# First column tile of a short-convolution layer: order of squares, low parts and scaling

## The chip, the cores and the metric

The kernel runs on one core of a Trainium2 chip. The metric is the device time of one execution in microseconds. The kernel before took 1109.05 us as the median of three runs (1108.74, 1109.05 and 1113.62). One more execution, recorded by the hardware profiler, took 1114.31 us; the rows below are from it.

## What is computed

A two-layer encoder step on 1088 tokens (1024 of a prompt, 64 of a running stream), with 1024 channels. The change lies in layer 0, the gated short convolution:

```python
h = rms_norm(x, norm_g[0])
b_gate, c_gate, xv, z = jnp.split(h @ w_in, 4, axis=-1)     # w_in: 1024 x 4096
u = c_gate * xv
conv = up[:, 0:T]*conv_w[0] + up[:, 1:1+T]*conv_w[1] + up[:, 2:2+T]*conv_w[2]   # up: two rows of state, then u
y = (silu(z) * b_gate * conv) @ w_out
```

Layer 1 is multi-head latent attention with a gate, and a last RMSNorm ends the step. Both come after the stretch that the change touches.

## The kernel before

Everything is held transposed: channels in the partitions, tokens in the columns. A float32 operand is split into a high part (rounded to the matmul's type, ACT) and a low part (source less high part); a product is three matmuls: high by high, high by low, low by high. Tokens come in two halves of 544 columns, and a half in two pieces, c=0 and c=1, of NS = 272 columns. The 4096 output columns of w_in are worked as eight column tiles `ct` of 128, each with four weight tiles of 128x1024, the parts, in the order 1, 2, 3, 0 (c_gate, xv, z, b_gate).

For the first half of the tokens, tiles 0, 1 and 2 are plain products (`conv_mm`, 24 matmuls for a part and a piece). `conv_mm` takes a `lag`: the matmuls with the weight's low part trail those with its high part by so many steps. From tile 3 on, two parts are taken together as a pair of seven block products of twelve matmuls (`Pair`, `prep`, `product`, `run`), which need sums and differences of the normalised x: `build(sc, k)` makes these, with VectorE and POOL for the first half (`sc` = 0, `build_first`) and POOL alone for the second.

The norm's factor is not applied to x before the first three tiles. x times the norm's gain is split (`x_split`), the squares of x are summed over the channels by `x_square` (ACT squares, VectorE adds into `rb`), and `rstd` sums `rb` over the partitions by TensorE (six matmuls of one column), takes the reciprocal root on VectorE in twelve small steps, and spreads it by TensorE (six matmuls of 128 columns); ACT copies it to `rb`, and `rb2` is its square. `finish_x` starts this and returns the rest of it. `conv_evac` scales a part by `rb2` or `rb` as it leaves PSUM; for the last part it goes on with `conv_tail`: three taps of the convolution in PSUM bank 7, then the gated result `y`, written to `y_scratch` by a DMA.

What sets the order: inside tile 0 ACT's, VectorE's and POOL's instructions that go through `ordered` are pinned behind what was traced before on their engine, and TensorE's matmuls are pinned from tile 0's first product on. DMAs (all on SP's queue), the weights of the next tiles, the builds and all that follows tile 0 on ACT, VectorE and POOL are placed by a scheduler that goes by the order of tracing and by when it takes an operand to be ready. Each engine then issues in that order. `side(n)` draws n steps from the list `jobs` (builds and `squares` of the second half): two after each piece in tiles 1 and 2, one after each block product in `run`.

PSUM has eight banks; `split_psum` deals them out and `gps` takes the next bank of a group in turn. In tile 0 group g has banks 0 to 6. A square goes to a buffer in SBUF (tags `kp6` and `cv`, the latter shared with `y`, one buffer each). The low parts of tile 0's weights are made by POOL. The scaling of piece c=0 stands behind the first product of c=1 as far as tracing goes, that of c=1 before tile 1. The second half's squares (`squares(k)` is four: channel tiles k and k+4 in two pieces, in two steps of two) go through bank 7: `squares(0)` and `squares(1)` in tiles 1 and 2, `squares(2)` and `squares(3)` ahead of `second_half` among the pairs. `second_half` lists at which of its 64 steps the second half's root and the four builds are drawn.

## Time and profile before

| | |
|---|---|
| median of three runs | 1109.05 us |
| profiled execution | 1114.31 us, its span 1112.5 us |
| PE busy | 1056.6 us (95%), 7123 matmuls |
| DVE, ACT, POOL busy | 749.8 (67%), 637.5 (57%), 539.7 us (49%) |
| PEclk in the first five of 40 slices | 8, 9, 9, 9, 8 tenths |
| DMA share in the first two slices | 7, 1 tenths |

PE is TensorE's matmuls, PEld its weight loads, DVE VectorE, ACT ScalarE, POOL GpSimd, SP the queue that issues the DMAs. Matmuls overlap at their ends, so PE's busy share is not the share of its peak. PEclk is the clock that TensorE was granted, as a share of the full one. In a timeline a row is: start, duration (of a run of like instructions from the first's start to the last's end), engine, line, operation, output and inputs, shapes, count, and in brackets the engine's idle time before it and what ended that.

### The profile page before, as it was taken

Reading aid. Unit: us, or ns where it says so; the run is one execution under the profiler, and the core shown is the slowest. Engines: PE = TensorE matmul, PEld = TensorE weight load, DVE = VectorE, ACT = ScalarE, POOL = GpSimd, SP = SyncE. Lnnn points to the kernel's source line nnn. Section 1 sums busy time; section 2 is a strip of 40 time slices with the busy share of each in tenths; the row PEclk is TensorE's granted clock in tenths of the full one; section 3 lists DMA queues with packets and bytes.
Section 4 is the critical chain, followed back from the end, with each engine's and each line's share of the span. In section 5 each row is a group of like instructions: output and inputs, shape, how many; then the busy total and the mean of one; then the engine's idle time right before and its main releaser. Section 6 shows DMA issues by size and latency. Waiting matters only on the chain.

```text
span 1112.5 us, 19655 instructions
## 1 busy us (share of the span) xinstructions
PE 1056.6 (95%) x7123; PEld 1010.2 (91%) x7123; DVE 749.8 (67%) x1516; ACT 637.5 (57%) x1388; POOL 539.7 (49%) x453
## 2 busy tenths in 40 slices
PE   8998899999999999999898999999999999999994
PEld 7888899999999999999798999899899999889983
DVE  6766577666666645564997432688888888896456
ACT  6445467666666533344532334777787777785352
POOL 3365399877666631221533321354555446463243
PEclk8999899999999999999999999999999999999997
DMA  7143234242322243422232104444323332334324
GB/s 233 59 136 107 82 115 141 86 164 77 114 96 96 95 140 131 139 82 87 92 122 98 51 31 107 100 98 96 83 57 88 86 74 49 100 124 152 93 83 153
DMA packets 58145, 114.55 MB, mean 103 GB/s; under 512 B 8080, under 2 KB 32400, under 8 KB 58048
## 3 DMA queue, kind: packets, MB, share of 16 engines
q1 hardware_dynamic: 57840, 112.97, 33.5%
q8 instruction: 56, 0.92, 0.4%
q14 instruction: 41, 0.34, 0.1%
q10 hardware_dynamic: 144, 0.26, 0.1%
q0 software_dynamic: 64, 0.07, 0.0%
HBM read 79.27 MB, written 16.31 MB: 86 GB/s over the span
## 4 chain that ended last, share of the span: by engine, by line
PE 66%; DVE 5%; issue 5%; POOL 4%; DMA 3%; ACT 3%; SPq 0%; POOLq 0%; ACTq 0%; DVEq 0%
PE PS L301 44%; PE PS L1459 17%; PE PS L1498 5%; DMA QB<-stg 2%; POOL wlo L1737 1%; DVE OL L983 1%; ACT PH L1511 1%; ACT stg L1575 1%; POOL t4l L632 0%; DMA wraw<-in_w 0%; POOL wlo L632 0%; SPq L1585 0%; DVE PL L1515 0%; DMA wraw<-in_wpair 0%; PE PS L1305 0%
## 5 line engine op out<-in xcount | busy, mean ns | idle before, releaser
L301 PE MATMUL PS<-R,whi 128*128 128x272 f32 (+2 forms) x1662 | 370.2, 312 | 16.6 <-DVE SZ L1003 5.2
L301 PEld LDWEIGHTS PS<-R,whi 128*128 128x128 f32 x1662 | 276.7, 191 | 21.5 <-ACT p L702 5.6
L301 PE MATMUL PS<-R,wlo 128*128 128x272 f32 (+2 forms) x888 | 266.7, 312 | 1.2 <-POOL wlo L292 0.9
L292 POOL TENSOR_TENSOR wlo<-wraw,whi 128x1024 fp32r<-128x1024 f32 x36 | 88.5, 2460 | 170.7 <-ACT whi L288 158.0
L301 PEld LDWEIGHTS PS<-R,wlo 128*128 128x128 f32 x888 | 165.1, 191 | 2.3 <-POOL wlo L292 1.7
L1459 PE MATMUL PS<-KB,QB 96*128 96x512 f32 (+11 forms) x576 | 126.6, 358 | 1.8 <-DMA QB<-stg 1.2
L1459 PEld LDWEIGHTS PS<-KB,QB 96*128 96x128 f32 (+1 forms) x576 | 95.5, 192 | 10.6 <-DMA QB<-stg 1.4
L1476 DVE TENSOR_REDUCE st<-PS 128x1 f32<-128x1024 f32 (+7 forms) x128 | 94.6, 748 | 13.1 <-PE PS L1459 12.3
L1493 POOL TENSOR_SCALAR Pt<-Pt,st 128x640 f32<-128x640 f32 (+3 forms) x64 | 61.4, 962 | 86.3 <-DVE st L1489 85.5
L1515 DVE TENSOR_TENSOR PL<-PS,PH 128x512 fp32r<-128x512 f32 (+3 forms) x192 | 98.7, 548 | 3.0 <-ACT PH L1511 1.6
L1511 ACT CAST PH<-PS 128x512 fp32r<-128x512 f32 (+3 forms) x192 | 85.4, 496 | 14.6 <-PE PS L1498 13.5
L1459 PE MATMUL PS<-PH,VB 128*128 128x256 f32 x320 | 76.4, 278 | 0.0
L632 POOL TENSOR_TENSOR wlo<-wraw,whi 128x1024 fp32r<-128x1024 f32 x26 | 62.4, 2401 | 26.7 <-ACT whi L631 24.0
L1459 PE MATMUL PS<-PL,VB 128*128 128x256 f32 x320 | 75.2, 281 | 0.2 <-DVE PL L1515 0.2
L1485 ACT ACTIVATE Pt<-PS,st 128x640 f32<-128x640 f32 (+3 forms) x64 | 62.1, 970 | 6.9 <-DVE st L1476 2.9
L301 PE MATMUL PS<-R,bhi 128*128 128x272 f32 x320 | 62.4, 293 | 2.3 <-DVE z L758 1.0
L1459 PEld LDWEIGHTS PS<-PH,VB 128*128 128x128 f32 x320 | 60.7, 190 | 1.3 <-DVE PL L1515 0.8
L1459 PEld LDWEIGHTS PS<-PL,VB 128*128 128x128 f32 x320 | 61.0, 190 | 0.7 <-DVE PL L1515 0.4
L288 ACT CAST whi<-wraw 128x1024 fp32r<-128x1024 f32 (+1 forms) x37 | 38.2, 1032 | 38.0 <-PE PS L301 20.4
L1498 PE MATMUL PS<-ident,Pt 128*128 128x128 f32 x416 | 55.4, 273 | 0.2 <-ACT Pt L1485 0.2
L301 PEld LDWEIGHTS PS<-R,bhi 128*128 128x128 f32 x320 | 50.5, 192 | 3.3 <-DVE u L758 1.4
L1493 POOL TENSOR_SCALAR Ph<-Ph,st 128x512 f32<-128x512 f32 (+3 forms) x64 | 34.0, 532 | 39.4 <-DVE st L1489 30.0
(438 smaller groups left out, 2649.9 us busy)
## 6 DMA issues: line engine op xcount, KB each, us to landing
wraw<-in_w SPq DMA_DIRECT2D x83, 512.0 KB, 3.5
KB<-stg SPq DMA_DIRECT2D x32, 256.0 KB, 3.8
QB<-stg SPq DMA_DIRECT2D x32, 256.0 KB, 5.1
braw<-in_w SPq DMA_DIRECT2D x13, 512.0 KB, 4.3
QB<-qr_scratch SPq DMA_DIRECT2D x32, 128.0 KB, 3.1
x<-x_scratch SPq DMA_DIRECT2D x8, 416.0 KB, 3.2
xr<-in_xT SPq DMA_DIRECT2D x16, 192.0 KB, 2.5
x_scratch<-xr SPq DMA_DIRECT2D x16, 192.0 KB, 1.8
```

What stands on the lines that cost most here:

```text
L288: ins = A.copy(out=hi[:, :n], in_=raw[:, :n])
L292: ins = (lo_engine or G).tensor_sub(lo[:, :m], raw[:, :m], r32(hi[:, :m]))
L301: ins = PE.matmul(ps, lhsT, rhs, start=start, stop=stop, skip_group_check=more)
L632: ins = eng.tensor_sub(lo, src, r32(hi))
L983: ordered((lo_engine or V).tensor_sub(lo, src, r32(hi)))
L1459: pin(PE.matmul(ps, lhsT, rhs, start=start, stop=stop))
L1476: pin(V.tensor_reduce(out=st[:, 0:1], in_=TL["S", h, i], axis=AX.XY, op=ALU.max, negate=True))
L1485: pin(A.activation(out=Pt, in_=TL.pop(("S", h, i)), func=AF.Exp, bias=st[:, 0:1], accum_out=st[:, 1:2]))
L1493: pin(G.tensor_scalar(Pt, Pt, st[:, 2:3], 1.0, op0=ALU.mult, op1=ALU.mult))
L1498: pin(PE.transpose(out=tp[:, j * P:(j + 1) * P], in_=TL["P", h, i][:, (j0 + j) * P:(j0 + j + 1) * P], identity=ident))
L1511: pin(A.copy(out=hi, in_=src))
L1515: pin(V.tensor_sub(lo, src, r32(hi)))
```

## The change

- The first tile's weights (all four parts) have their low part made by VectorE in place of POOL.
- A square of x goes to PSUM: bank group q (banks 6 and 7), and group g has banks 0 to 5. `rstd` in tile 0 uses q as well.
- Tile 0 is written out: the squares of c=0 are dealt between the casts of the third and fourth weight and after them; x of c=1 is loaded and split before any c=1 product; squares of c=1 come after the scaling of c=0's first two parts. The third product of c=0 and the fourth have the low parts at the end (lag KD).
- The spread of c=0 is put halfway into the second product of c=1 (`mid`), the scaling of c=0 comes in two portions behind it, and root, spread and scaling of c=1 (`rest`) come behind the first product of tile 1. Tile 1 takes its `u` and `z` after that.
- `y` has two buffers.
- `squares(2)` moves from the pairs to tiles 1 and 2; `squares(3)` has four steps of one square in place of two of two.
- The second half's root ends one step later, and its four builds start one step later at a spacing of 12 steps in place of 13.
- `os_` (attention, later) lies in pool pz in place of const.

```diff
--- before.py
+++ after.py
@@ -281,7 +281,7 @@
         if cuts:
             def part(a, b):
                 ordered(A.copy(out=hi[:, a:b], in_=raw[:, a:b]))
-                ordered(G.tensor_sub(lo[:, a:b], raw[:, a:b], r32(hi[:, a:b])))
+                ordered((lo_engine or G).tensor_sub(lo[:, a:b], raw[:, a:b], r32(hi[:, a:b])))
             return hi, lo, lambda a, b: SP.dma_start(out=raw[:, a:b], in_=src[:, a:b]), part
         dst = raw[:, :n] if view is None else view(raw[:, :n])
         SP.dma_start(out=dst, in_=src)
@@ -429,22 +429,22 @@
         return (STG, ST2)[k % 4 // 2][:, o:o + SC]
 
     def x_dma(c, k):
-        XS[k] = staged(k)[:, c * NS:(c + 1) * NS]
-        SP.dma_start(out=XS[k], in_=xT[k][:, c * NS:(c + 1) * NS])
+        XS[c, k] = staged(k)[:, c * NS:(c + 1) * NS]
+        SP.dma_start(out=XS[c, k], in_=xT[k][:, c * NS:(c + 1) * NS])
 
     def x_split(c, k):
         c0, c1 = c * NS, (c + 1) * NS
         g = sm[:, C_NG + k:C_NG + k + 1]
-        ordered(A.activation(out=HS[:, k, c0:c1], in_=XS[k], func=AF.Copy, scale=g))
-        ordered(V.scalar_tensor_tensor(LS[:, k, c0:c1], XS[k], g, r32(HS[:, k, c0:c1]), op0=ALU.mult, op1=ALU.subtract))
+        ordered(A.activation(out=HS[:, k, c0:c1], in_=XS[c, k], func=AF.Copy, scale=g))
+        ordered(V.scalar_tensor_tensor(LS[:, k, c0:c1], XS[c, k], g, r32(HS[:, k, c0:c1]), op0=ALU.mult, op1=ALU.subtract))
 
     def x_square(c, k):
         c0, c1 = c * NS, (c + 1) * NS
         if k == 0:
-            ordered(A.activation(out=rb[:, c0:c1], in_=XS[k], func=AF.Square))
+            ordered(A.activation(out=rb[:, c0:c1], in_=XS[c, k], func=AF.Square))
         else:
-            q = p1.tile([P, NS], F32, tag=("kp6", "cv")[k % 2], name=nm("sq"), bufs=1)
-            ordered(A.activation(out=q, in_=XS[k], func=AF.Square))
+            q = gps("q")[:, :NS]
+            ordered(A.activation(out=q, in_=XS[c, k], func=AF.Square))
             ordered(V.tensor_add(rb[:, c0:c1], rb[:, c0:c1], q))
 
     def load_x(c, ks=range(KD)):
@@ -455,7 +455,7 @@
 
     def finish_x(c):
         c0, c1 = c * NS, (c + 1) * NS
-        end = rstd([rb[:, c0:c1]], rb[:, c0:c1], D, NS)
+        end = rstd([rb[:, c0:c1]], rb[:, c0:c1], D, NS, tag="q")
 
         def rest():
             end()
@@ -463,12 +463,14 @@
 
         return rest
 
-    def conv_mm(c, W, lag=0):
+    def conv_mm(c, W, lag=0, mid=None):
 
         cs = slice(c * NS, (c + 1) * NS)
         wh, wl = W
         ps = gps()[:, :NS]
         for k in range(KD + lag):
+            if k == KD // 2 and mid:
+                mid()
             if k < KD:
                 mm(ps, wh[:, k * P:(k + 1) * P], HS[:, k, cs], k == 0, False)
                 mm(ps, wh[:, k * P:(k + 1) * P], LS[:, k, cs], False, False)
@@ -492,7 +494,7 @@
             A.activation(out=cv[:, s], in_=us[:, ct, 0:2], func=AF.Copy, scale=cw[0])
             for j in (1, 2):
                 V.scalar_tensor_tensor(cv[:, s], us[:, ct, j:j + 2], cw[j], cv[:, s], op0=ALU.mult, op1=ALU.add)
-        y = p1.tile([P, NS], F32, tag="cv", name=nm("y"), bufs=1)
+        y = p1.tile([P, NS], F32, tag="cv", name=nm("y"), bufs=2)
         ordered(V.tensor_mul(y, cv, z[:, a:b]))
         c0, c1 = sc * SC + a, sc * SC + b
         if sc == 0:
@@ -600,7 +602,10 @@
                 else:
                     A.activation(out=t, in_=q, func=AF.Square)
                     V.tensor_add(s, s, t)
-            yield
+                if k == 3:
+                    yield
+            if k < 3:
+                yield
 
     jobs = []
 
@@ -788,14 +793,14 @@
     PARTS = [1, 2, 3, 0]
     STD = 3
     pairs = [f for sc, cts in ((0, range(STD, KD)), (1, range(KD))) for ct in cts for f in conv_pairs(ct, sc)]
-    split_psum(g=(0, 7))
+    split_psum(g=(0, 6), q=(6, 8))
     ahead = []
     for ct in range(STD):
-        u, z = new_u(ct, 0), new_z()
         if ct == 0:
+            u, z = new_u(ct, 0), new_z()
             W = {}
             keep_order[0] = True
-            *w, dma, part = load_w(w1[ct][PARTS[0]], 1024, cuts=True)
+            *w, dma, part = load_w(w1[ct][PARTS[0]], 1024, lo_engine=V, cuts=True)
             W[PARTS[0]] = w
             dma(0, 256)
             x_dma(0, 0)
@@ -809,41 +814,58 @@
             part(640, 1024)
             for k in range(2, KD):
                 x_split(0, k)
-            *w, dma, part = load_w(w1[ct][PARTS[1]], 1024, cuts=True)
+            *w, dma, part = load_w(w1[ct][PARTS[1]], 1024, lo_engine=V, cuts=True)
             W[PARTS[1]] = w
             dma(0, 1024)
             part(0, 512)
             part(512, 1024)
             pe_order[0] = True
             held = {c: [] for c in range(2)}
-            held[0].append(conv_mm(0, W[1], 3))
-            for part, ks in ((3, range(4)), (0, range(4, KD))):
-                for k in ks:
+
+            def first(c, pi, lag=0, mid=None):
+                held[c].append(conv_mm(c, W[PARTS[pi]], lag, mid))
+
+            def evac(c, *pis):
+                for pi in pis:
+                    conv_evac(0, u, z, PARTS[pi], c, held[c][pi])
+
+            first(0, 0, 3)
+            for i, part in enumerate((3, 0)):
+                W[part] = load_w(w1[ct][part], 1024, lo_engine=V, into=[p1.tile([P, 1024], F32R, tag=x, name=nm(x), bufs=1) for x in ("bhi", "blo")] if part else
+                                 [R1[:, REG - n:REG - n + 1024] for n in (2048, 1024)])
+                for k in range(2 * i, 2 * i + 2):
                     x_square(0, k)
-                W[part] = load_w(w1[ct][part], 1024, into=[p1.tile([P, 1024], F32R, tag=x, name=nm(x), bufs=1) for x in ("bhi", "blo")] if part else
-                                 [R1[:, REG - n:REG - n + 1024] for n in (2048, 1024)])
-            for c in range(2):
-                for pi, part in enumerate(PARTS):
-                    if c or pi:
-                        held[c].append(conv_mm(c, W[part], (0, 6, 8, 0)[pi] if c == 0 else 0))
-                    late = c == 0
-                    if pi == 1 + late:
-                        n = 4 if late else 0
-                        if late:
-                            load_x(1, range(n))
-                        end = finish_x(c)
-                        if late:
-                            load_x(1, range(n, KD))
-                    if pi == 2 + late:
-                        end()
-                        for q in range(3):
-                            conv_evac(ct, u, z, PARTS[q], c, held[c][q])
-                    if pi == 3:
-                        conv_evac(ct, u, z, part, c, held[c][3])
+            first(0, 1, 6)
+            for k in range(KD):
+                x_dma(1, k)
+            for k in range(4, KD):
+                x_square(0, k)
+            first(0, 2, KD)
+            first(0, 3, KD)
+            for k in range(KD):
+                x_split(1, k)
+            end = finish_x(0)
+            first(1, 0)
+            first(1, 1, 0, end)
+            evac(0, 0, 1)
+            for k in range(4):
+                x_square(1, k)
+            first(1, 2)
+            for k in range(4, KD):
+                x_square(1, k)
+            evac(0, 2, 3)
+            first(1, 3)
+            end = finish_x(1)
+
+            def rest(u=u):
+                end()
+                evac(1, 0, 1, 2, 3)
+                conv_state(0, 0, u)
+
             keep_order[0] = False
-            split_psum(g=(0, 5))
+            split_psum(g=(0, 5), q=(7, 8))
             turns["g"][1] = 2
-            jobs.extend([build_first(0), build_first(1), squares(0), build_first(2), squares(1), build_first(3)])
+            jobs.extend([build_first(0), build_first(1), squares(0), build_first(2), squares(1), build_first(3), squares(2)])
         else:
             for pi, part in enumerate(PARTS):
                 W = ahead.pop() if ahead else load_w(w1[ct][part], 1024)
@@ -851,12 +873,18 @@
                     ahead.append(load_w(w1[ct + (pi == 3)][PARTS[(pi + 1) % 4]], 1024))
                     paced["lo"] = lo_on[0]
                 for c in range(2):
-                    conv_evac(ct, u, z, part, c, conv_mm(c, W, (KD, 0)[c]))
+                    ps = conv_mm(c, W, (KD, 0)[c])
+                    if ct == 1 and pi == c == 0:
+                        rest()
+                    if pi == c == 0:
+                        u, z = new_u(ct, 0), new_z()
+                    conv_evac(ct, u, z, part, c, ps)
                     side(2)
                 if ct == STD - 1:
                     with tc.issue_after(lo_on[0]), tc.issue_after(hi_on[0]):
                         step(0, (0, 1, 1, 4)[pi])
-        conv_state(ct, 0, u)
+        if ct:
+            conv_state(ct, 0, u)
     while jobs:
         side()
 
@@ -870,19 +898,19 @@
             todo.setdefault(t, []).append(f)
 
         def factors():
-            todo[8] = [rstd([rb[:, SC:]], rb[:, SC:], D, SC)]
+            todo[9] = [rstd([rb[:, SC:]], rb[:, SC:], D, SC)]
 
         at(3, factors)
         for k in range(4):
             steps = build(1, k)
-            for t in (0, 5, 6, 13):
-                at(10 + 13 * k + t, lambda steps=steps: next(steps, None))
+            for t in (0, 5, 6, 12):
+                at(11 + 12 * k + t, lambda steps=steps: next(steps, None))
         for t in range(64):
             for f in todo.get(t, []):
                 f()
             yield
 
-    jobs.extend([squares(2), squares(3), second_half()])
+    jobs.extend([squares(3), second_half()])
     step(1)
 
     pairs[2 * (KD - STD)].whole = True
@@ -1261,7 +1289,7 @@
 
     PSH = pS.tile([P, 5, 2 * P], F32R, name="PSH")
     PSL = pS.tile([P, 5, 2 * P], F32R, name="PSL")
-    os_ = const.tile([P, 8, DEC], F32, name="os_")
+    os_ = pz.tile([P, 8, DEC], F32, name="os_")
 
     WV, QA, PT, OL = {}, {}, {}, {}
```

## Rows read from the trace of the kernel before

**Rows 1.** Stretches: us, then busy us (instructions) by engine, clock, DMA share, GB/s.

```profile
12.80:45.85 33.05, 27.87 (x195) 26.83 (x194) 24.20 (x61) 17.44 (x38) 12.88 (x8) 0.90 0.40 136
45.85:97.35 51.50, 49.41 (x384) 48.30 (x385) 35.09 (x70) 23.83 (x44) 33.03 (x20) 1.00 0.38 114
97.35:121.30 23.95, 18.41 (x109) 17.75 (x108) 15.10 (x41) 10.04 (x21) 6.80 (x4) 0.79 0.29 101
131.00:223.00 92.00, 89.14 (x693) 88.29 (x692) 62.38 (x126) 61.65 (x119) 79.74 (x56) 0.98 0.33 116
150.00:200.00 50.00, 49.87 (x397) 49.61 (x396) 35.56 (x70) 35.23 (x68) 47.73 (x34) 1.00 0.39 130
```

**Rows 2.** Timeline, PE, first tile.

```profile
23.36 5.35 PE L301 MATMUL PS<-R 128*128 128x272 f32 x22 [1.55 <-POOL R L292]
...
35.66 0.72 PE L301 MATMUL PS<-ones,acc 128*128 128x1 f32 x6
...
41.43 0.93 PE L301 MATMUL PS<-ident,rsy 128*128 128x128 f32 x6 [1.93 <-DVE rsy L333]
```

**Rows 3.** PE's waits, 0 to 130 us: us in total, times, longest.

```profile
PE PS L301 <- ACT p L702: 3.9, 2, 2.8
PE PS L301 <- DVE rsy L333: 1.9, 1, 1.9
PE PS L301 <- DVE acc L602: 1.6, 1, 1.6
PE PS L301 <- POOL R L292: 1.5, 1, 1.5
PE PS L301 <- DVE acc L448: 1.2, 1, 1.2
```

**Rows 4.** Timeline, ACT and DVE, first tile.

```profile
11.91 1.14 ACT L283 CAST whi<-wraw 128x512 fp32r<-128x512 f32 x2 [2.09 <-DMA wraw<-in_w]
...
13.73 6.83 DVE L448 TENSOR_TENSOR acc<-acc,sq 128x272 f32<-128x272 f32 x7 [2.80 <-ACT sq L447]
...
25.82 0.15 DVE L323 TENSOR_SCALAR rsv<-PS 128x3 f32<-128x3 f32 x1
...
27.98 0.16 DVE L333 SCALAR_TENSOR_TENSOR rsy<-rst,rsy 128x3 f32<-128x3 f32 x1
```

**Rows 5.** Instructions by form, DVE, 0 to 42 us: count, busy us, mean ns, idle before.

```profile
L448 DVE TENSOR_TENSOR acc<-acc,sq 128x272 f32<-128x272 f32 x14 | 9.2, 659 | 3.4 <-ACT sq L447 2.8
```

**Rows 6.** Instructions by form, DVE, 42 to 98 us.

```profile
L602 DVE TENSOR_TENSOR acc<-acc,PS 128x272 f32<-128x272 f32 x6 | 2.6, 432 | 1.5 <-ACT PS L601 1.4
...
L563 DVE TENSOR_TENSOR R<-STG,R 128x544 fp32r<-128x544 f32 x2 | 1.4, 714 | 0.0
...
L574 DVE TENSOR_TENSOR R<-STG,R 128x272 fp32r<-128x272 f32 x2 | 0.9, 433 | 0.0
```

**Rows 7.** Instructions by form, POOL, 0 to 42 us.

```profile
L292 POOL TENSOR_TENSOR wlo<-wraw,whi 128x1024 fp32r<-128x1024 f32 x2 | 4.8, 2392 | 10.6 <-ACT whi L288 10.6
```

**Rows 8.** Timeline, first and last steps of the first half's builds.

```profile
43.18 0.78 DVE L568 SCALAR_TENSOR_TENSOR STG<-STG,sm,acc 128x544 f32<-128x544 f32 x1
...
89.43 1.38 POOL L563 TENSOR_TENSOR R<-ST,R 128x544 fp32r<-128x544 f32 x1 [3.02 <-ACT R L562]
```

**Rows 9.** Timeline, first pairs: DVE, ACT, PE.

```profile
104.64 0.44 DVE L496 TENSOR_TENSOR y<-PS,z 128x272 f32<-128x272 f32 x1 [2.45 <-DMA y_scratch<-y]
...
105.12 0.40 ACT L601 ACTIVATE PS<-ST 128x272 f32<-128x272 f32 x1 [3.57 <-DVE u L540]
106.02 0.40 ACT L601 ACTIVATE PS<-ST 128x272 f32<-128x272 f32 x1 [0.50 <-DVE acc L602]
...
107.69 0.58 PE L301 MATMUL PS<-R,whi 128*128 128x272 f32 x2 [2.82 <-ACT p L702]
```

**Rows 10.** Timeline, second half's builds: ACT and PE.

```profile
201.27 0.42 ACT L573 CAST R<-ST 128x272 fp32r<-128x272 f32 x1 [4.20 <-POOL ST L571]
...
205.91 0.52 PE L301 MATMUL PS<-R,whi 128*128 128x272 f32 x2 [1.80 <-ACT p L702]
```

## The prediction

> **What bounds the kernel now.** The busy shares (in the table) name TensorE, so the question is where TensorE loses time and who releases it. I read the stretches first [rows 1]. Between 150 and 200 us it runs 397 matmuls in 49.87 us, 0.126 us for one: that is the pace with nothing in the way. Three stretches are held against it.
> 12.80 to 45.85 us (first column tile from its second weight on): 195 matmuls, 168 of them long, 168 x 0.126 = 21.2 us; the other 27 are two sets of column sums and two of spreads at 0.72 and 0.93 us [rows 2] and the first three of the next tile, about 3.3 us. So 24.5 us of work stands in 33.05 us: 8.6 us lost.
> 45.85 to 97.35 us (tiles 1 and 2): 384 x 0.126 = 48.4 in 51.50: 3.1 lost.
> 97.35 to 121.30 us (first seven-product pairs): 109 matmuls, 99 long ones 12.5 us and ten sums about 0.8, so 13.3 in 23.95: 10.6 lost.
> The waits [rows 3] give the releasers. In the first tile: the accumulated squares (1.2 us), the low part of the fourth weight by POOL (1.5) and the reciprocal root of half c=1 (1.9). At the pairs: ACT's copies of finished products (3.9) and again the squares (1.6). The rest is clock: the 22 matmuls at 23.36 took 5.35 us, 0.243 each [rows 2], nearly twice the pace, behind 1.55 us of idle; between 97.35 and 121.30 the granted clock was 0.79 [rows 1]. Of the 10.6 us there 3.9 + 1.6 = 5.5 are waits, so 5.1 is clock: a wait costs about itself once more.
> After that the matmuls run at pace until the next stage, so what TensorE gains before 125 us is kept if nothing else becomes late.
>
> **First tile, 12.80 to 45.85 us.** The start stays: the second weight is cast at 11.91, after 2.09 us of waiting for its transfer [rows 4], and TensorE can't begin on it before about 12.6. x tiles of c=1 follow both later weights on SP's queue, as before, so no transfer is put ahead of one that is needed sooner.
> Squares: seven adds took 6.83 us from 13.73 [rows 4], 0.98 each, while POOL made low parts. The mean of all 14 is 0.659 us [rows 5]; the same sum with the square in PSUM (later in the kernel) takes 0.432 [rows 6].
> The Trainium skill (SBUF — State Buffer, Who interferes with whom) has it that a VectorE instruction with two SBUF inputs and a GpSimd one that reads SBUF exclude each other, and that one with a single SBUF input is free of it; the two rows agree. The rule also speaks against this change: low parts and the product for rb2 have two SBUF inputs, so the latter could stand behind a POOL low part of the next tile (2.39 us), and the sum below would be smaller by up to that.
> Low parts: POOL needs 2.39 us for 128x1024 [rows 7]. VectorE at that size isn't in the trace. 0.714 us for 544 columns and 0.433 for 272 [rows 6] make a slope of 1.03 ns a column, so 0.714 + 480 x 0.00103 = 1.21 us; bounds are 0.71 (544 columns) and 2.39 (POOL's). I take 1.21, the straight line. Two halves of the second weight and three pieces of the first cost VectorE about 2.9 us more together, the third and fourth weight 2.4.
> VectorE's queue then: second weight's low halves to 13.9, third's to 15.4, one add, fourth's to about 17.2, six adds to 19.8, eight low parts of x(c=1) at about 0.45 (the 272-column subtraction of [rows 6]) to 23.5. TensorE needs: second weight 12.8 to 15.8, third to 18.8, fourth to 21.8 (low parts from 20.8), sums to 22.5, then x(c=1) piece k at 22.5 + 0.38k against 20.3 + 0.45k. Nothing is late, so the 1.2, the 1.5 and the slow 22 matmuls (22 x 0.117 = 2.6 us) go. If VectorE needed 2.39 a low part, the fourth would end near 20.5 and the adds near 23.1: the sums 1.3 us late.
> The reciprocal root: from 25.82 to 27.98 [rows 4], 2.3 us on VectorE. For c=0 it runs under first(1,0) and half of first(1,1), 36 x 0.126 = 4.5 us: hidden. New wait: first(1,2) takes bank 0 again, which is free only after spread, copy, rb2 and the first scaling, some 0.2 + 0.4 + 0.45 + 0.45 behind the spread against 1.5 us of remaining matmuls: 0.6 us of wait with semaphores. For c=1 the sums come after first(1,3) and the spread after the next tile's first 24 matmuls (3.0 us). VectorE reaches that chain only behind the gated result of c=0 (a table load, SiLU, POOL's product, three taps), about 40.4 against 39.7: 0.8 us of wait. Queued behind the waiting VectorE steps are the scalings of c=1 and the first builds; TensorE has five banks, and asks for the first that they hold some 12 us later.
> So 24.5 + 0.6 + 0.8 = 25.9 in place of 33.05: **-7** (-3.3 to -8.5; the near end takes 1.3 for slow low parts and one POOL low part of 2.39 in front of rb2, as POOL stood in front of the adds in [rows 4]).
>
> **Tiles 1 and 2.** The builds of the first half need rb of c=1. Before, the first came at 43.18, 2.7 us ahead of tile 1, and the last of POOL's at 89.43 to 90.8 [rows 8], 6.5 us ahead of the pairs at 97.35. Now tile 1 starts near 36.7 and rb is there near 42: the builds stand some 8 us later against TensorE, and the second product, which needs the last of them, had 9 us to spare (about 99.9 less 90.8). Four squares of half two come in as well, 4 x 0.432 on VectorE and 4 x 0.40 on ACT. VectorE had 35.09 us of work in 51.50 [rows 1], some of it waiting for POOL, so there is room to catch up, but the cover is nearly used. Bounds: 0 (all hidden) and +8 (the chain of builds keeps its length). I take **+1.5**, near the free end because of the idle share.
>
> **First pairs, 97.35 to 121.30 us.** VectorE waited 2.45 us with y at 104.64 for the transfer of the y before (one buffer); ACT's next square waited 3.57 us behind it, more squares each for the add before, and the copy that TensorE needed came behind these: 2.82 us idle at 107.69 [rows 9]. With two buffers y doesn't wait. Four squares, not eight, are left, one a product (1.5 us) and not two (some 0.9 us each through one bank, from 105.12 to 106.02): they fit. The sums then find their adds done. What stays is the 1.07 us of the first copy (3.9 - 2.82), since in the first pair only one product lies between the two that use its bank, and perhaps 2 us for squares whose x arrives just in time. 10.6 - 1.1 - 2 = 7.5: **-7.5** (-3 to -9.5).
>
> **Half two's builds, 131 to 223 us.** POOL was busy 79.74 of 92 us [rows 1]; 16 low parts of 2.4 leave 41.3, 10.3 a build. At 13 products a build (19.7 us, with 8.9 of low parts) POOL just kept up; at 12 (18.1 us against 10.3 + 8.2 = 18.5) it falls behind by 0.4 a build, but ends three products sooner, before the next half asks. One such lag shows: ACT's cast waited 4.20 us for POOL, and TensorE 1.80 for a copy behind it [rows 10]. It may go or come twice: **+0.5** (-3.5 to +5). The later reciprocal root (one step) and os_ in another pool move no work: 0. Two y buffers let half two's POOL reads trail: 0 to -1, taken as 0.
>
> **Sum.** -7 + 1.5 - 7.5 + 0.5 = -12.5. The profiled execution took 1114.31 us (span 1112.5 and 1.81 around it), so its like would take 1101.8. The median of the three runs is 5.26 under it, so the forecast is 1109.05 - 12.5 = 1096.5 us.
>
> **Rivals.** (a) The builds keep their length, and the pairs wait for them at about the old hour: +8 in place of +1.5, -6, 1103. For: most of it is a chain over three engines. Against: VectorE's idle third. (b) The copies at the pairs stay late, now behind squares whose x is reloaded after the last build: -2 in place of -7.5, -7, 1102. For: ACT issues in order. Against: half the squares. (c) Both: -0.5, 1108.5. (d) The change doesn't do what it says in the first tile: the third and fourth weight land too late for TensorE and it idles as before, -1 for -7: 1102.5. Against: ACT before cast them behind waits for adds, not for transfers. (e) Slower: POOL over-full in half two's builds. Each cast that waits for POOL holds ACT's copies; one cost 1.8 us of wait and, by the ratio above, 1.7 of clock, 3.5. There are 16 such casts (four a build). From the sixth further one (6 x 3.5 - 12.5 = +8.5) the kernel is at 1117.5. For: 0.4 us a build too much; against: low parts are made a pair ahead.
>
> **Chances.** Forecast 0.56 (own range 1090 to 1101), (a) 0.13, (b) 0.11, (c) 0.08, (d) 0.06, (e) 0.06. The range takes in (a), (b) and (d) and reaches below the forecast for the full losses (-8.5 - 9.5 - 3.5): 1088 to 1106. About what a measurement of this kernel can tell from no change is 0.5%, 5.5 us: below 1103.5 lies the forecast and most of (a), (b) and (d): faster 0.77; same 0.16, (c) with the rest of these; slower 0.07.
>
> **What would show it.** First tile: adds at 0.43 each, no POOL low part before about 25 us, full clock from 13 to 40, next tile's first matmul near 37. Tiles 1 and 2: no wait for a build; the pairs' first matmul near 91. Pairs: no wait of y for a transfer, clock near 1.0 after. Builds: at most one or two waits for a copy. Wrong would be a first matmul of the pairs after 95, a slow clock behind it, or more than four waits for copies from 125 to 215.

## The result, and the profile after

The changed kernel took 1099.2 us (median of 7 runs, 1096.45 to 1102.93); the kernel before took 1114.73 on the same chip (7 runs, 1108.74 to 1116.55). The ratio is 0.9877, 95% interval 0.9845 to 0.9909: faster by about 1.2%. The profiled spans are 1097.4 and 1112.5 us, a difference of 15.1; the sum had said 12.5. From the median of 1109.05 that was shown ahead, the ratio gives 1095.4 us, beside the 1096.5 forecast. (1109.05 lay at the lower end of the runs before; in the later comparisons the kernel before has medians of 1109.86 to 1111.94.)

To see where the time came from, both traces are laid side by side by their matmuls. Each has 7123, issued in the same places of the program at the numbers below, so the start of the n-th one is a common clock:

```
n                                     after     before   after - before
72    (first tile, early)             15.41      16.01       -0.60
300   (tile 1 under way)              45.00      53.42       -8.42
624   (the pairs begin)               93.91      97.35       -3.44
800   (pairs' sums are done)         118.38     131.51      -13.13
1000                                 143.44     158.17      -14.73
1300                                 185.51     195.93      -10.42
1500  (half two's builds are done)   210.72     224.71      -13.99
7122  (last)                        1090.89    1106.01      -15.12
```

So the first tile gave 7.8 us (from -0.60 to -8.42), tiles 1 and 2 took 5.0 back, the pairs gave 9.7, half two's builds 0.9. The first 0.6 and the last 1.1 are not put down to the change: among the traces of this case the 72nd matmul starts anywhere from 14.81 to 17.80 us, with the landing of the first transfers and the clock behind it, and from the 3500th matmul (near 500 us) to the last the traces of the experiments below shift against that of the changed kernel by -1.9 to +6.1 us, though their edits lie before.

The stretches that answer to [rows 1], first tile, tiles 1 and 2, pairs, builds and the part of them at pace (us; busy us and instructions of PE, PEld, DVE, ACT, POOL; granted clock, DMA share, GB/s):

```profile
12.30:36.40 24.10, 23.46 (x187) 23.25 (x188) 17.96 (x44) 16.20 (x33) 5.55 (x3) 1.00 0.57 197
36.40:93.85 57.45, 51.67 (x391) 50.02 (x391) 46.89 (x93) 26.48 (x52) 35.75 (x20) 0.97 0.33 104
93.85:108.75 14.90, 13.43 (x108) 13.21 (x108) 13.34 (x34) 8.84 (x18) 6.90 (x4) 1.00 0.45 146
117.00:209.00 92.00, 88.90 (x700) 87.72 (x699) 63.49 (x128) 62.79 (x120) 79.72 (x56) 1.00 0.33 117
136.00:186.00 50.00, 46.90 (x365) 45.80 (x364) 32.72 (x67) 34.76 (x66) 44.72 (x34) 1.00 0.34 119
```

The first tile and the pairs stand at a granted clock of 1.00, where the pairs had 0.79, and TensorE fills them to nine tenths and more. The middle stretch is the one to read: 391 matmuls at 0.126 us are 49.3 us and it lasts 57.45, so 8.2 us are lost where 3.1 were. VectorE's busy time there went from 35.09 to 46.89 us, with 93 instructions for 70: root and scaling of c=1 and four more squares stand there now.

TensorE's waits to 130 us, against [rows 3] (us in total, times, longest):

```profile
PE PS L301 <- ACT whi L288: 4.4, 3, 2.8
PE PS L301 <- ACT p L707: 1.5, 1, 1.5
PE PS L301 <- POOL wlo L292: 1.2, 3, 0.5
...
PE PS L301 <- DVE u L528: 0.6, 1, 0.6
...
PE PS L301 <- DVE rsy L333: 0.2, 1, 0.2
```

All five waits of [rows 3] are gone but one copy and a short spread. Grown are the waits for a cast weight (`whi`, ACT; 1.0 us in two before) and for POOL's low part behind it (0.9 in two before). They stand in tiles 1 and 2. In the timeline (start, duration, instruction, in brackets the idle time before it and what ended it) TensorE, ACT, VectorE and POOL show this around the longest of them:

```profile
64.43 3.48 PE L301 MATMUL PS<-R,whi 128*128 128x272 f32 x16 [2.81 <-ACT whi L288]
...
60.01 0.42 ACT L575 CAST R<-ST 128x272 fp32r<-128x272 f32 x1 [4.85 <-DVE ST L570]
...
63.34 1.04 ACT L288 CAST whi<-wraw 128x1024 fp32r<-128x1024 f32 x1
...
53.31 1.60 DVE L576 TENSOR_TENSOR R<-STG,R 128x272 fp32r<-128x272 f32 x1
54.84 2.91 DVE L565 TENSOR_TENSOR R<-STG,R 128x544 fp32r<-128x544 f32 x1
57.67 1.60 DVE L579 TENSOR_TENSOR STG<-STG 128x272 f32<-128x272 f32 x1
59.20 0.77 DVE L570 SCALAR_TENSOR_TENSOR ST<-ST,sm,acc 128x544 f32<-128x544 f32 x1
...
53.10 1.52 POOL L565 TENSOR_TENSOR R<-STG,R 128x544 fp32r<-128x544 f32 x1 [4.15 <-ACT R L564]
54.59 2.57 POOL L292 TENSOR_TENSOR wlo<-wraw,whi 128x1024 fp32r<-128x1024 f32 x1
57.13 1.85 POOL L565 TENSOR_TENSOR R<-STG,R 128x544 fp32r<-128x544 f32 x1
```

Read it from the bottom. POOL works without a gap from 53.10 to 58.98 us. VectorE starts a two-input build step beside each of POOL's three instructions and each time ends it only 0.3 to 0.6 us behind POOL's end: 1.60, 2.91 and 1.60 us for sizes that took 0.43 and 0.71 [rows 6]. So the next build step (`ST`, L570) comes only at 59.20; ACT has waited 4.85 us for it; the next weight's cast is issued behind that build's copies on ACT and begins at 63.34; TensorE stands 2.81 us, and its next 16 matmuls run at 0.218 us each. The cast itself was ready long before: its weight had landed at 35.92, and the last matmul on the buffer that it writes ended at 55.6. What holds it is its place in ACT's order. In the stretch (instructions by form, count, busy us, mean ns):

```profile
L576 DVE TENSOR_TENSOR R<-STG,R 128x272 fp32r<-128x272 f32 x2 | 4.3, 2129 | 0.0
...
L565 DVE TENSOR_TENSOR R<-STG,R 128x544 fp32r<-128x544 f32 x2 | 3.6, 1813 | 0.0
```

Against [rows 6] (433 and 714 ns) these four instructions alone take 5.6 us more. Over all of VectorE's instructions that start between 36 and 92 us, the time beyond the shortest instruction of the same operation and shape (its excess, below) is 11.4 us; between 42 and 98 us of the kernel before it was 6.2 (the expectations below give 11.0 and 6.0).

In the first tile, POOL, DVE and PE show what was forecast, against [rows 2, 4, 5]:

```profile
16.72 3.14 DVE L448 TENSOR_TENSOR acc<-acc,PS 128x272 f32<-128x272 f32 x6
...
27.86 1.15 DVE L462 TENSOR_TENSOR rb2kp<-acc 128x272 f32<-128x272 f32 x1 [2.46 <-ACT acc L346]
...
26.33 2.39 POOL L292 TENSOR_TENSOR wlo<-wraw,whi 128x1024 fp32r<-128x1024 f32 x1 [25.01 <-ACT whi L288]
...
18.41 3.16 PE L301 MATMUL PS<-R 128*128 128x272 f32 x24
21.40 0.73 PE L301 MATMUL PS<-ones,acc 128*128 128x1 f32 x6
...
29.54 0.52 PE L301 MATMUL PS<-R,bhi 128*128 128x272 f32 x2 [0.64 <-DVE u L528]
```
```profile
L448 DVE TENSOR_TENSOR acc<-acc,PS 128x272 f32<-128x272 f32 x14 | 6.1, 436 | 1.2
...
L292 DVE TENSOR_TENSOR blo<-wraw,bhi 128x1024 fp32r<-128x1024 f32 x1 | 1.2, 1226 | 0.4 <-ACT bhi L288 0.4
```

The adds take 436 ns for 659, POOL's first low part comes at 26.33, the 24 matmuls at 18.41 run at the pace, and the column sums follow without a gap at 21.40. The wait at 29.54 is that of c=1's third product, `first(1, 2)`, for the scaling that stands right behind the product for `rb2` (L462).

At the pairs and in half two's builds, against [rows 9, 10]:

```profile
99.06 0.43 DVE L498 TENSOR_TENSOR y<-PS,z 128x272 f32<-128x272 f32 x1
...
98.55 0.52 PE L301 MATMUL PS<-R,t2h 128*128 128x272 f32 x2 [1.47 <-ACT p L707]
...
104.69 1.17 PE L301 MATMUL PS<-ones,acc 128*128 128x1 f32 x10
```
```profile
166.25 0.42 ACT L575 CAST R<-ST 128x272 fp32r<-128x272 f32 x1 [4.25 <-POOL ST L573]
...
170.87 0.52 PE L301 MATMUL PS<-R,whi 128*128 128x272 f32 x2 [1.87 <-ACT p L707]
```

`y` waits for no transfer, the sums find their adds done, and the one stall of the builds has moved from the fourth build (205.91) to the third (170.87) with nearly the same size.

### The profile page after: what moved, and what is told of

It is laid out like the page before. It is cut to its first block, busy times and chain, and to the rows that moved or that the text cites. A ratio compares the mean times of both kernels' runs of the same rounds, so it can differ in the third digit from the quotient of the medians.

```text
span 1097.4 us, 19670 instructions
## 1 busy us (share of the span) xinstructions
PE 1048.0 (95%) x7123; PEld 1003.3 (91%) x7123; DVE 754.0 (69%) x1523; ACT 638.3 (58%) x1388; POOL 532.1 (48%) x446
## 4 chain that ended last, share of the span: by engine, by line
PE 69%; DVE 10%; POOL 5%; issue 5%; DMA 4%; ACT 4%; SPq 1%; POOLq 0%; DVEq 0%; ACTq 0%
PE PS L301 48%; PE PS L1487 16%; PE PS L1526 5%; DMA QB<-stg 3%; POOL wlo L1765 1%; DMA wraw<-in_w 1%; POOL wlo L292 1%; DVE PS L488 1%; ACT PH L1539 1%; DVE OL L1011 1%; ACT stg L1603 1%; POOL R L565 1%; SPq L1613 1%; DVE PL L1543 0%; POOL R L513 0%
## 5 line engine op out<-in xcount | busy, mean ns | idle before, releaser
L1568 POOL TENSOR_TENSOR SZ<-SZ,ot 64x256 f32<-64x256 f32 x64 | 47.0, 746 | 11.7 <-DVE ot L1563 9.4
```

Of the source, the lines that this page charges most:

```text
L1568: pin(G.tensor_mul(sz, sz, TL.pop(("ot", h, pr))[rows]))
```

## The experiments

Each kernel is the changed kernel with the edit shown. Two measures are given: the ratio to the kernel before, measured beside it on the same chip (95% interval; the changed kernel itself stands at 0.9877), and, finer, how much later than in the changed kernel the n-th matmul starts, counted from n = 72 so that the first transfers drop out. In us, for the kernel before and for each run:

```
                   n=300    624    800   1500
kernel before       7.82   2.84  12.52  13.39
lo_pool             0.01   0.03  -0.04   0.00
sq_sbuf             3.30   1.50   1.47   1.51
lo_pool_sq_sbuf     4.15   4.12   4.06   4.07
scale_at_end        5.61   3.96   4.08   4.05
y_one               0.02   0.07   1.74   3.50
sq_pairs            0.00  -0.18   6.76   6.79
y_one_sq_pairs      0.00  -0.18   8.59  10.26
casts_first         0.02   0.38   0.42   0.44
builds_later        0.00  -1.35   6.59   6.75
spacing_13          0.29   0.28   0.76   1.51
no_low_read        -0.67  -7.60  -7.81  -7.75
low_halves          0.18  -0.86  -0.54  -0.53
```

Where an edit can't have acted yet (n = 300 for y_one, sq_pairs, y_one_sq_pairs and spacing_13), the rows differ by up to 0.3 us, so differences of that size are not read.

### First tile: low parts, squares, scaling

**lo_pool**, the low parts of the first tile back on POOL:
```diff
-            *w, dma, part = load_w(w1[ct][PARTS[0]], 1024, lo_engine=V, cuts=True)
+            *w, dma, part = load_w(w1[ct][PARTS[0]], 1024, cuts=True)
...
-                W[part] = load_w(w1[ct][part], 1024, lo_engine=V, into=...
+                W[part] = load_w(w1[ct][part], 1024, into=...
```


> The changed kernel with the first tile's low parts back on POOL; squares stay in PSUM and the order stays. Theory (the two-input conflict): adds read one SBUF operand and stay at 0.43 us, so POOL's low parts (2.39 us each) only hold up the low parts of x. The fourth weight's low part is then ready near 20 us against 20.8 needed: second sums (35.69 us in the changed kernel) 0.5 to 2 us later, total +0.5 to +2. Rival (POOL's speed itself was the loss, 1.5 us of wait and the slow clock behind it): the wait for POOL at the fourth weight comes back, second sums 4 us later or more, total +4.


Measured: 1098.33 us, ratio 0.9896 (0.9862 to 0.9929). The n-th matmuls stand within 0.04 us. With the squares in PSUM, POOL's low parts don't lengthen the adds:

```profile
L448 DVE TENSOR_TENSOR acc<-acc,PS 128x272 f32<-128x272 f32 x14 | 6.1, 437 | 6.6 <-ACT PS L447 5.4
```

Both expectations were too high: this part of the change is worth nothing by itself.

**sq_sbuf**, squares in SBUF, low parts still on VectorE:
```diff
-            q = gps("q")[:, :NS]
+            q = p1.tile([P, NS], F32, tag=("kp6", "cv")[k % 2], name=nm("sq"), bufs=(1, 2)[k % 2])
```


> The changed kernel with the squares of x written to SBUF as before (two tags), low parts on VectorE. Theory (conflict): no POOL instruction runs before 26 us, so the seven adds of piece c=0 keep 0.43 to 0.5 us and nothing moves before 29 us; the adds of c=1 (29.9 to 33.6 us) meet POOL's low part of the next tile (29.95 to 32.35) and end about 2 us later, which moves the second root and its spread (39.72 us) by 1 to 2 us: total +1 to +2. Rival (the buffers in PSUM were the gain): first sums (21.40 us) 2 us later or more.


Measured: 1101.55 us, ratio 0.9909 (0.9881 to 0.9937). The seven adds of c=1 take 5.72 us (timeline), one of them 2.46 beside POOL's low part of a weight of tile 1:

```profile
30.19 5.72 DVE L448 TENSOR_TENSOR acc<-acc,sq 128x272 f32<-128x272 f32 x7
```

and the spread of c=1 is late (TensorE's waits, us in total, times, longest):

```profile
PE PS L301 <- DVE rsy L333: 2.0, 1, 2.0
```

3.3 us at n = 300, of which tiles 1 and 2 absorb all but 1.5.

**lo_pool_sq_sbuf**, both edits.


> Both of the above in one: only the new order of the first tile is left of its edits. Theory (conflict): adds of c=0 run beside POOL's low parts again, 0.9 us each, first sums 3 us later or more than in the changed kernel, slow clock behind it, second sums 4 to 6 us later: more than the two alone together. Rival (order alone is the gain): second sums within 1.5 us of the changed kernel's.


Measured: 1103.13 us, ratio 0.9937 (0.9915 to 0.9959). 4.1 us, where the two alone make 0 + 1.5: the two edits meet on one conflict, and it takes both sides, an add with two SBUF inputs and a POOL instruction beside it. The timeline of the adds of c=0, and TensorE's waits for the spreads, now two:

```profile
15.94 6.58 DVE L448 TENSOR_TENSOR acc<-acc,sq 128x272 f32<-128x272 f32 x6 [0.73 <-ACT sq L447]
```
```profile
PE PS L301 <- DVE rsy L333: 4.1, 2, 2.2
```

Six adds take 6.58 us, as seven took 6.83 in [rows 4]. Either half of the change removes the conflict of c=0; only the squares in PSUM also remove that of c=1, where POOL belongs to the next tile. The new order, which is all that is left of the first tile's edits here, is worth 3.7 us at n = 300 (7.82 less 4.15).

**scale_at_end**, root, spread and scaling of c=1 at the end of tile 0:
```diff
+            rest()
...
-                    if ct == 1 and pi == c == 0:
-                        rest()
```


> The changed kernel with root, spread and scaling of c=1 put at the end of the first tile, ahead of tile 1's first product. Theory: TensorE waits for the root there, 36.4 to 39.5 us, so about 3 us less 0.2 that it waits now: tile 1's 24 first matmuls end 2.5 to 3 us later; total +1 to +3, since tiles 1 and 2 lose 6 us later to ACT's late weight casts and may lose less then. Rival: the order of the rest shifts with it and takes all of it back, 0.


Measured: 1103.39 us, ratio 0.993 (0.9906 to 0.9954). The spread then stands ahead of tile 1's first product on TensorE and waits for the root (TensorE's waits):

```profile
PE PS L301 <- DVE rsy L333: 3.3, 1, 3.3
```

5.6 us at n = 300, 4.0 kept, more than the 1 to 3 expected: a wait of 3.3 and the clock behind it (0.72 granted from 38 to 50 us). The deferral is the largest single piece of the first tile's gain.

### The pairs: `y` and the squares

**y_one**, one buffer for the gated result:
```diff
-        y = p1.tile([P, NS], F32, tag="cv", name=nm("y"), bufs=2)
+        y = p1.tile([P, NS], F32, tag="cv", name=nm("y"), bufs=1)
```


> The changed kernel with one buffer for y. Theory 1 (the wait of y for the transfer of the y before starts the stall at the pairs): the wait of about 2.4 us is back on VectorE near 101 us and TensorE idles 1.5 to 3 us behind it, with slow clock: total +3 to +5. Theory 2 (the number of squares between the copies makes the stall): y's wait is back, but TensorE loses less than 1 us.


Measured: 1102.36 us, ratio 0.9921 (0.9898 to 0.9944). y waits, and TensorE for a copy behind it (timeline, DVE and PE):

```profile
101.94 0.44 DVE L498 TENSOR_TENSOR y<-PS,z 128x272 f32<-128x272 f32 x1 [1.67 <-DMA y_scratch<-y]
...
104.09 0.52 PE L301 MATMUL PS<-R,whi 128*128 128x272 f32 x2 [1.15 <-ACT p L707]
```

1.7 us at the pairs, less than the first theory's 3 to 5 but with its wait. As much again is lost near 200 us, still among the first half's pairs, where y waits once more (1.65 us) and TensorE 1.48 for a scaling behind it.

**sq_pairs**, the squares of the second half at their old place and two a step, y with two buffers:
```diff
-                if k == 3:
-                    yield
-            if k < 3:
-                yield
+            yield
...
-            jobs.extend([..., squares(1), build_first(3), squares(2)])
+            jobs.extend([..., squares(1), build_first(3)])
...
-    jobs.extend([squares(3), second_half()])
+    jobs.extend([squares(2), squares(3), second_half()])
```


> The changed kernel with squares(2) and squares(3) ahead of the second half's steps as before, two squares a step; y keeps two buffers. Theory 1: the stall at the pairs stays away, total 0 to +2 there, and tiles 1 and 2 lose up to 1 us less without squares(2). Theory 2: ACT's copies stand behind two squares a product again, TensorE waits 3 us or more with slow clock, the pairs' first 100 matmuls take 19 us or more in place of 14.9: total +4 to +6.


Measured: 1106.34 us, ratio 0.9945 (0.9926 to 0.9965). 6.8 us, all at the pairs. PE's timeline, and the stretch in the columns of the first fence:

```profile
108.97 1.97 PE L301 MATMUL PS<-ones,acc 128*128 128x1 f32 x10 [3.15 <-DVE acc L604]
```
```profile
93.85:116.00 22.15, 17.36 (x112) 16.71 (x111) 15.72 (x41) 9.96 (x21) 7.41 (x4) 0.85 0.31 109
```

This is the second theory, and somewhat beyond its size. TensorE waits chiefly for the last add, ahead of the column sums, less for copies (1.6 us, for 1.5 in the changed kernel); the mean clock is 0.85 where it was 1.00.

**y_one_sq_pairs**, both edits.


> Both undone: the pairs as before, the first tile as changed. By either theory the 9 us at the pairs come back, in part or whole (pairs' first 100 matmuls near 24 us in place of 14.9), total +5 to +9; if they do not come back, the pairs' gain came from the first tile's shift and not from these two edits.


Measured: 1107.87 us, ratio 0.9978 (0.9958 to 0.9997). 8.6 us at n = 800, the sum of the two (1.7 + 6.8). Counted from n = 624 it is 8.8 of the 9.7 us that the pairs gained; 0.9 is not accounted for by these two. With both edits undone TensorE's waits here are again chiefly for copies (3.5 us in two, 1.7 for the last add), as in [rows 3].

### Tiles 1 and 2: why 5 us came back

**casts_first**, the weight's cast issued ahead of the build steps on ACT:
```diff
-                    paced["lo"] = lo_on[0]
+                    paced["lo"], paced["hi"] = lo_on[0], hi_on[0]
```


> An addition to the changed kernel: in tiles 1 and 2 the ACT instructions of builds and squares are issued behind the cast of the weight that was loaded ahead. Theory (the 6 us lost in tiles 1 and 2 come from casts of weights queued on ACT behind build steps that wait for VectorE): waits of TensorE for these casts (4.4 us now) and for the low parts behind them (1.2) fall under 1.5 us together, the pairs start 3 to 6 us earlier (near 89 to 91 us in place of 93.9), total -2 to -6. Rival (the builds themselves are the bound): the casts come earlier, but the pairs wait for builds, total within 1 us.


Measured: 1100.86 us, ratio 0.9909 (0.9889 to 0.9929), 0.4 us slower by the matmuls, about what can't be read. The expected 2 to 6 us didn't come: TensorE still waits for casts (and 2.0 us, for 1.2, for the low parts behind them), and ACT now stands idle in front of SiLU for VectorE's scaling (TensorE's waits from 39 to 95 us, then two lines of ACT's timeline):

```profile
PE PS L301 <- ACT whi L288: 3.0, 2, 2.3
```
```profile
61.42 0.43 ACT L533 ACTIVATE z<-z 128x272 f32<-128x272 f32 x1 [5.55 <-DVE z L532]
...
63.50 1.04 ACT L288 CAST whi<-wraw 128x1024 fp32r<-128x1024 f32 x1
```

VectorE is late here too. But the theory isn't refuted: the edit holds back only steps that are drawn after the weight's load, and the cast at 63.50, only 0.5 us earlier than in the changed kernel (counted from n = 72), still stands behind that SiLU, two build casts and two squares drawn before it. Its weight had landed at 36.80 and its buffer was free at 56.35, so it could have run in ACT's 5.55 us of idle time. A cast put ahead of that SiLU was not tried.

**no_low_read**, the low parts of the weights of tiles 1 and 2 left out: POOL writes zeros of the same size in their place, and so reads no SBUF:
```diff
-        ins = (lo_engine or G).tensor_sub(lo[:, :m], raw[:, :m], r32(hi[:, :m]))
+        ins = G.memset(r32(lo[:, :m]), 0.0) if zero else (lo_engine or G).tensor_sub(...)
```


> The changed kernel, but the low parts of the weights of tiles 1 and 2 are left out: POOL writes zeros there and reads no SBUF for them (these tiles' products are of lower precision). Theory (the 6.6 us lost in tiles 1 and 2: VectorE's two-input build steps stand still beside POOL's low parts, 11.0 us over their shortest durations between 36 and 92 us against 6.0 before, which makes the scalings late and ACT's SiLU and weight casts behind them): that excess falls under 5 us, TensorE waits under 1.5 us there and the pairs start 4 us earlier or more. Rival (VectorE has too much work or a bad order, POOL or not): the casts are still waited for, the pairs start less than 2 us earlier.


Measured: one run, 1089.68 us. The stretch from n = 300 to 624 shrinks by 6.9 us; first VectorE's and POOL's instructions by form (36 to 92 us), then TensorE's waits (36 to 98 us), then a line of VectorE's timeline in the first tile:

```profile
L576 DVE TENSOR_TENSOR R<-STG,R 128x272 fp32r<-128x272 f32 x2 | 2.0, 1022 | 0.0
...
L565 DVE TENSOR_TENSOR R<-STG,R 128x544 fp32r<-128x544 f32 x2 | 1.4, 714 | 0.0
...
L292 POOL MEMSET wlo<- 128x1024 f32 x6 | 5.7, 953 | 3.1 <-PE PS L301 3.1
```
```profile
PE PS L301 <- ACT whi L288: 1.3, 1, 1.3
```
```profile
28.47 0.44 DVE L462 TENSOR_TENSOR rb2kp<-acc 128x272 f32<-128x272 f32 x1 [2.49 <-ACT acc L346]
```

The 544-column step is back at 714 ns, one of the two 272-column steps is still long (mean 1022), and the waits for low parts are gone. So POOL's making of low parts, beside the builds, is what these 7 us hang on. How is less clear. VectorE's excess is 6.2 us, not under 5 as expected, and no less than in the kernel before. The zeros also cost POOL less than half (953 ns, for 2542 in the changed kernel) and don't wait for the cast, so this run alone doesn't say whether VectorE's standing still or POOL's own queue counts for more.

The run also settles a point of the first tile. With no POOL low part beside it the product for `rb2` takes 0.44 us for 1.15, the wait of `first(1, 2)` (0.64 us) is gone, and the 300th matmul comes 0.67 us earlier.

**low_halves**, the same low parts in two instructions of 512 columns each:
```diff
+        for a in range(0, m, m // pieces):
+            b = a + m // pieces
+            ins = (lo_engine or G).tensor_sub(lo[:, a:b], raw[:, a:b], r32(hi[:, a:b]))
...
-                W = ahead.pop() if ahead else load_w(w1[ct][part], 1024)
+                W = ahead.pop() if ahead else load_w(w1[ct][part], 1024, pieces=2)
```


> The changed kernel with POOL's low parts of the weights of tiles 1 and 2 made in two instructions of 512 columns (1.39 us each by the rows of the kernel before) in place of one of 1024 (2.39). Theory (a VectorE build step stands still until the POOL instruction beside it ends): the step waits for half as long; the excess over the shortest durations between 36 and 92 us falls from 11.0 to about 8, the weight casts come 2 to 3 us earlier, pairs start 1.5 to 4 us earlier, total -1 to -4. Rival (POOL and VectorE take turns, so the total of both stays and POOL is the later one): VectorE's excess falls, but TensorE waits for the low parts instead, total within 1 us or slower.


Measured: 1099.74 us, ratio 0.9894 (0.9873 to 0.9915), 0.9 us earlier at n = 624 and 0.5 at n = 800, where 1.5 to 4 was expected. The two forms that stood still longest are short again (2129 and 1813 ns in the changed kernel), but others stand still more (the first line below, 1088 ns in the changed kernel), and the excess falls only from 11.4 to 8.5 us. First VectorE by form (36 to 92 us), then TensorE's waits, which hardly fell (36 to 98 us):

```profile
L572 DVE SCALAR_TENSOR_TENSOR ST<-ST,sm,acc 128x544 f32<-128x544 f32 x4 | 5.9, 1474 | 0.0
...
L578 DVE TENSOR_TENSOR R<-STG,R 128x272 fp32r<-128x272 f32 x2 | 2.0, 987 | 0.0
...
L567 DVE TENSOR_TENSOR R<-STG,R 128x544 fp32r<-128x544 f32 x2 | 1.4, 718 | 0.0
```
```profile
PE PS L303 <- ACT whi L288: 4.1, 3, 2.4
...
PE PS L303 <- POOL wlo L294: 1.6, 1, 1.6
```

It doesn't beat the changed kernel by more than can be measured.

**builds_later**, the builds' steps held back beside the first weight of tile 1 (both products):
```diff
-                    side(2)
+                    if ct > 1 or pi:
+                        side(2)
```


> The changed kernel with the first four build steps (two draws beside tile 1's first part) drawn one part later; 26 steps have 28 places. Theory (builds that are traced early but ready late stand ahead of the scalings on VectorE): the scaling of tile 1's third part, 7.6 us late now, comes within 3 us of its product, the wait of 2.8 us for the weight cast goes, pairs start 2 to 5 us earlier. Rival (the builds' own length is the bound): waits move to the end of tile 2 or to the first pairs, total within 1.5 us.


Measured: 1107.47 us, ratio 0.997 (0.9949 to 0.999). The pairs begin 1.35 us earlier and then lose 7.9: one copy is 4.8 us late there (TensorE's waits from 95 us on, then the last build step on VectorE):

```profile
PE PS L301 <- ACT p L707: 4.8, 1, 4.8
```
```profile
93.19 1.91 DVE L565 TENSOR_TENSOR R<-ST,R 128x544 fp32r<-128x544 f32 x1
```

The rival had the place right, the first pairs, and the size wrong: 6.6 us at n = 800 and not within 1.5. The run mixes two things. The last build step ends 1.7 us behind the pairs' first matmul, where POOL's last ended 6.5 us ahead of it in the changed kernel; and `squares(2)` slips among the pairs with the builds, so that eight squares stand there and not four, as in sq_pairs, which lost 6.8 us without any late build. So what late builds cost by themselves is not shown.

### Half two's builds

**spacing_13**, root and builds of half two at the old steps:
```diff
-            todo[9] = [rstd([rb[:, SC:]], rb[:, SC:], D, SC)]
+            todo[8] = [rstd([rb[:, SC:]], rb[:, SC:], D, SC)]
...
-            for t in (0, 5, 6, 12):
-                at(11 + 12 * k + t, lambda steps=steps: next(steps, None))
+            for t in (0, 5, 6, 13):
+                at(10 + 13 * k + t, lambda steps=steps: next(steps, None))
```


> The changed kernel with root and builds of the second half at their former steps (8; start 10, spacing 13). Theory (POOL is full there, the spacing only moves the place of its backlog): the loss of 4.3 us between the 1000th and the 1300th matmul shrinks and one of 2 to 4 us near the 1370th comes back; pairs of the second half start within 1.5 us of the changed kernel's. Rival (12 ends the builds sooner and saves the last stall): they start 2 to 4 us later.


Measured: 1100.95 us, ratio 0.9908 (0.9872 to 0.9943). 0.76 us at n = 800, 1.51 at n = 1500, of which 0.3 stands at n = 300 already: about 1.2; in between it is 2.4 us behind at n = 1000 and 1.9 ahead at n = 1300. As the theory had it, the single stall of some 1.8 us moves from one build to another and isn't removed by either spacing.

## Why the prediction was right

**Right in the time, and in mechanism at the first tile and the pairs; one term was mis-sized.** The sum was -12.5, the profiled spans differ by 15.1; without the start and the stages behind the builds, where no term lay, 13.4. That the sum came so near is partly luck: the terms missed by -0.8, +3.5, -2.2 and -1.4, which nearly cancel. The terms:

```
                     forecast  (bounds)         measured
first tile             -7      -3.3 to -8.5       -7.8
tiles 1 and 2          +1.5     0   to +8         +5.0
first pairs            -7.5    -3   to -9.5       -9.7
half two's builds      +0.5    -3.5 to +5         -0.9
```

- **First tile.** The adds at 436 ns, no POOL low part before 25 us, the granted clock of 1.00 and tile 1's first matmul near 37 came out as said. VectorE's 128x1024 low part took 1.226 us; the straight line from the 272- and 544-column rows gave 1.21. The spread's new wait was 0.21 us for 0.8. That of `first(1, 2)` was 0.64 for 0.6, but by luck: the forecast's own steps (0.2 + 0.4 + 0.45 + 0.45 against 1.5) leave no wait, no row gives its 0.6, and the measured wait has another cause (next point). The forecast gave part of the gain to VectorE's low parts, and that was wrong: with the squares in PSUM they are worth 0.0 us (lo_pool). Where the squares are in SBUF they are worth 2.6 (4.1 less 1.5), and the deferral of c=1's scaling is worth 4.0 by itself.
- The product for rb2 (L462) began at 27.86, behind POOL's low part of 26.33, and took 1.15 us where the nearest row of that size has 0.43 [rows 6]; POOL's instruction ended at 28.72. That is the Trainium skill's rule (SBUF — State Buffer, Who interferes with whom: with both inputs in SBUF, VectorE's instruction and GpSimd's reads exclude each other). By it the sum was to be smaller by up to 2.39; the trace agrees on the mechanism, with 0.7 us. TensorE lost nearly all of it: the scaling behind rb2 ended at 29.49, `first(1, 2)` began at 29.54 after 0.64 us of wait, and without POOL's reads that wait is gone (no_low_read).
- **Tiles 1 and 2: the mis-sized term.** The step of the forecast was "I take +1.5, near the free end because of the idle share". An idle third of VectorE said little, because what makes a VectorE step long here is POOL beside it and not VectorE's load. The builds begin 1 us earlier by the hour (42.17 for 43.18 us), but TensorE is 8.4 ahead, so they stand some 7 us later against it. So they and the low parts of the weights that TensorE asks for next fall together, and one late scaling makes a late SiLU, a late cast and a late product. Of 8.2 us lost, 5.6 are waits (4.4 and 1.2), the rest mostly clock (0.97 granted over 57.45 us, about 1.7). This is a part of rival (a), of whose +8 it makes five eighths, but not by its mechanism: the pairs didn't wait for the builds' chain, whose last step ended 6.5 us ahead of them as before; the weights did. Shown: without POOL's making of the low parts the stretch is 6.9 us shorter (no_low_read). Open: how these 7 us split between VectorE standing still, POOL's queue and ACT's order. Halving POOL's instructions took 2.8 us of VectorE's excess away and gave 0.9; leaving the low parts out took 5.2 away, and with them POOL's queue, and gave 6.9. That speaks for POOL's queue having a part, but no run parts the two. Casts put ahead of the SiLU that waits for VectorE are an untested remedy (casts_first doesn't do it).
- **Pairs.** More than said, and by the mechanism named: y's wait went, the sums found their adds done, the clock stayed at 1.00. The first copy's wait stayed (1.47 us for 1.07). The 2 us allowed for squares on reloaded x didn't come. The forecast had the copies as the larger loss; with the squares alone put back it is the wait for the sums (3.15 us) and the clock behind it, with y's buffer undone as well it is the copies (3.5 us), as forecast.
- **Half two's builds.** One wait for a copy in place of one, within "at most one or two"; rival (e), from six on, didn't come near.

Of the signs listed ahead, the one that pointed to trouble was the pairs' first matmul: 91 was forecast, 95 would have been wrong, 93.91 came.

## What to carry to other kernels

Where POOL and VectorE both work on SBUF, read the mean duration of each VectorE form beside POOL and away from it before counting VectorE's idle share as room: the 272-column subtractions of the builds went from 0.43 us to a mean of 2.13. Where a wait is removed early in a pipeline, ask which prepared work (builds, casts, low parts) loses its lead against TensorE, and price that as a queue, not as a sum of durations. Of several edits to one conflict, one may carry the whole gain; undoing them singly and together tells which.

## What the runs showed of the hardware

- Starts of matmuls with the same number agree within 0.3 us between executions until an edit acts, once the start (the 72nd matmul at 14.81 to 17.80 us) is taken out. That made effects of 1 us readable by the trace, far below what whole times with their 3 to 10 us of spread allow.
- A wait costs more than itself: in sq_pairs 3.15 us for the sums, with copies as in the changed kernel but for 0.1, became 6.8 us at the pairs (granted clock 0.85 in the stretch), and in scale_at_end a wait of 3.3 us for the spread 5.6 at n = 300.
